# A decoder layer's projection weights laid out by the host in chunks of 256 columns, and a sixth raw buffer for them

## The chip, the cores and the metric

The kernel runs on one core of one Trainium2 chip. The metric is device time in microseconds (us), the median of several executions. Engine names are those of the profile: PE does the matmuls (PEld loads their stationary operand), DVE, ACT and POOL work on tiles, SP issues plain DMAs, and POOL issues the indirect DMAs (the gathers). SPq and POOLq are the queues of these issues.

## What is computed

One decoder layer for 512 tokens of width 1024, cut to what matters here:

```python
z = rmsnorm(x) @ w_in                    # 1024 x 3592, split into:
# ml_qk 1024 | ml_v 512 | ml_o 512 | ml_i 4, ml_f 4 | da_q 512 | da_k 512 | da_v 512
h = concat([mlstm_heads(...), diff_attention_heads(...)])     # 4 heads of each
x = x + h @ w_out
# cross-attention into a memory of 256 rows
q = rmsnorm(x) @ w_cq;  k = mem_n @ w_ck;  v = mem_n @ w_cv
x = x + softmax(q k^T / 16) v @ w_co
# PEER: each token takes 16 of 16384 experts for each of 8 heads
q = rmsnorm(x) @ w_pq;  sc = q . sub_keys;  eidx, gate = product_key_top16(sc)
x = x + sum_k gate_k * gelu(h . peer_u[eidx_k]) * peer_v[eidx_k]
out = rmsnorm(x)
```

All of w_out, w_cq, w_ck, w_cv, w_co and w_pq are 1024 x 1024, in float32.

## The kernel before

The tokens are four blocks of 128. The program runs in groups:

- The **first group** is block 0 alone, up to about 220 us: input projection (`proj_feat` and `proj_tok` with `w_in`; tiles qkg, vg, og, dag, dvg), mLSTM and attention, `mem_front` (keys and values of the memory; tiles mkw, mvw), output projection (wog), cross-attention (cqt, co0) and the PEER query (pq0).
- The **second group** is `mixers(1, 3, ...)`, blocks 1 to 3 together, from about 226 to 640 us. Beside it block 0's experts are fetched and reduced: POOL gathers rows of `peer_u` and `peer_v` (512 KB each, tiles u and v), and DVE takes the dot products with u and the weighted sums of v. `feed` mixes them into the projections.
- The **tail** (640 to some 800 us) does cross-attention and the PEER query for blocks 2, 3 and 1; routing follows. From 1000 us on, blocks 2 and 3 go through all experts as dense matmuls (tiles ud, vd, of 512 and 256 KB), block 1 by gathers.

The projection weights are read from HBM as the model stores them, rows of the full matrix. `w_parts` (line 337) brings one chunk of 256 columns in two halves of 512 KB, [128 partitions, 4, 256], where each partition gets 4 runs of 1 KB that lie a whole matrix row apart, 128 rows each. The raw halves go round a ring of buffers, `rings["wr"]`: 5 in the first group, 3 in the second. A load of a half can be issued once the half that was in its buffer has been used. Where a product is split for precision, ACT casts the half to a rounded H (line 346), DVE or POOL subtract it for L (line 330), and PE runs three matmuls for one (lines 314 to 316); elsewhere PE multiplies the raw half (line 322). In the tail `w_chunk` (line 219) brings a chunk of 1 MB at once, 8 runs of 1 KB for each partition, in another ring.

All these loads, the loads of constants and of x, and the stores of intermediate results to HBM go through SP's one queue, in order. The constants of `setup_small` are among them: lt (line 254) holds the four lambda vectors, each broadcast to 128 partitions; its two products ljunk (line 258) run on DVE ahead of eo (line 510). The memory's values are stored in mv_d (line 446).

The order on each engine is not written out by hand. The framework's scheduler builds it, from dependencies, free buffers and its own estimate of durations; the program only gives the order in which instructions are handed to it, and rings of buffers.

Of the kernel before, what the change touches and what calls it, by code (L numbers as in the profile page):

```python
# [19 lines left out]
P = 128  # L20
S = 512
D = 1024
ND = 8
# [64 lines left out]
def layer_kernel(ctx, tc, x, mem, norm_mix_g, w_in, conv_w, b_igate, b_fgate, ml_norm_g,  # L88
                 lambda_q1, lambda_k1, lambda_q2, lambda_k2, da_norm_g, w_out, norm_ca_g,
                 norm_mem_g, w_cq, w_ck, w_cv, w_co, norm_ffn_g, w_pq, sub_keys, peer_u, peer_v,  # L90
                 final_norm_g, peer_ut, out):

# [1 line left out]

    nc = tc.nc
    xf = x[0]
    w_in, w_out, w_cq, w_ck, w_cv, w_co, w_pq = (a[0] for a in (w_in, w_out, w_cq, w_ck, w_cv, w_co, w_pq))
    uf = peer_u[0]  # L100
    vf = peer_v[0]
    outf = out[0]
# [17 lines left out]
    def pa(name):  # L120
        return psums[1](name)
# [46 lines left out]
    mp = fctx.enter_context(tc.tile_pool(name="mixers", bufs=1, side="right"))  # L168
    actx = ExitStack()
    home = [actx.enter_context(tc.tile_pool(name="first", bufs=1, side="right"))]  # L170
    rings = {"big": 4, "wr": 5, "wH": 2, "wL": 2}

    def ft(shape, tag, name, bufs=2, dt=F32):
        return home[0].tile(shape, dt, tag=tag, name=name, bufs=bufs)
# [39 lines left out]
    def w_tile(shape, name):  # L214
        return ft(shape, "w", name, bufs=rings["w"])

    def w_chunk(src, c0, name):
        t = w_tile([P, ND, 256], name)
        nc.sync.dma_start(t, src[:, c0:c0 + 256].rearrange("(k p) c -> p k c", p=P))
        return t  # L220

    def load_x(src, T0, NT, name):
# [14 lines left out]
    cols = bp.tile([P, 64], F32, name="cols")  # L237
    nc.vector.tensor_copy(cols, cps[:, :64])
    wg = mp.tile([P, ND, 8], F32, name="wg")
    nc.sync.dma_start(wg, w_in[:, 2048:2056].rearrange("(k p) c -> p k c", p=P))  # L240
    wgs = tuple(mp.tile([P, ND, 8], F32R, name=f"wg{hl}") for hl in "HL")
    put(wgs, wg)

# [82 lines left out]
    def low(dst, src, high):  # L326
        kind = LOW[min(lows[0], len(LOW) - 8 + lows[0] % 8)] if group[0] else LOW_FIRST[lows[0] % 8]
        lows[0] += 1
        e = nc.gpsimd if kind == "pool" else nc.vector
        e.tensor_sub(dst, src, high.bitcast(F32))  # L330

    def w_parts(src, c0, name, split):

        for q in range(2):
            sh = [P, 4, 256]
            raw = ft(sh, "wr", f"{name}_{q}", bufs=rings["wr"])
            nc.sync.dma_start(raw, src[q * 512:(q + 1) * 512, c0:c0 + 256].rearrange("(k p) c -> p k c", p=P))
            if not split:
                yield range(4 * q, 4 * q + 4), raw
                continue  # L340
            if group[0] or rings["wH"] and lows[0] % 2:
                H = ft(sh, "wH", f"{name}H{q}", bufs=rings["wH"], dt=F32R)
            else:
                H = keep.tile(sh, F32R, tag="hv", name=f"{name}H{q}", bufs=2)
            L = ft(sh, "wL", f"{name}L{q}", bufs=rings["wL"], dt=F32R)
            nc.scalar.copy(H, raw)
            low(L, raw, H)
            yield range(4 * q, 4 * q + 4), (H, L)
# [43 lines left out]
    def proj_feat(src, c0, nf, T, n, name, evac, parts=w_parts):  # L392

        for c in range(nf // 2):
            o = [pa(f"{name}o{c}{j}") for j in range(2)]
            for ks, w in parts(src, c0 + c * 256, f"{name}w{c}", T.split):
                for j in range(2):
                    for k in ks:
                        product(o[j][:, :n], at(w, slice(None), k - ks[0], slice(j * P, (j + 1) * P)), T(k),
                                k == 0, k == ND - 1)  # L400
                    if ks[-1] == ND - 1:
                        evac(2 * c + j, o[j][:, :n])
            feed("proj", n // P)

    def proj_tok(src, c0, n, T, NT, name, evac, parts=w_parts):

        for c in range(0, n, 256):
            o = [pa(f"{name}o{c}_{tt}") for tt in range(NT)]
            for ks, w in parts(src, c0 + c, f"{name}w{c}", T.split):
                for tt in range(NT):  # L410
                    for k in ks:
                        product(o[tt][:, :256], T(k, slice(tt * P, (tt + 1) * P)), at(w, slice(None), k - ks[0]),
                                k == 0, k == ND - 1)
                    if ks[-1] == ND - 1:
                        evac(tt, c, o[tt][:, :256])
            feed("proj", NT)
# [38 lines left out]
    def mixers(T0, NT, hT):  # L455
        G = NT * P
        g = f"g{T0}_"
# [100 lines left out]
        def ev_da(f, o):  # L558
            if f < 4:
                nc.scalar.mul(daqT[:, f, :], o, -0.125)  # L560
            else:
                nc.scalar.copy(dakT[:, f - 4, gl], o)
        proj_feat(w_in, 2056, 8, hT, G, f"da{g}", ev_da)

        def ev_dv(tt, c, o):
            nc.scalar.copy(dav[:, T0 + tt, c:c + 256], o)
        proj_tok(w_in, 3080, 512, hT, NT, f"dv{g}", ev_dv)

        mix = big([P, NT, D], f"mix{g}")

# [483 lines left out]
    for tt in range(NDENSE):  # L1054
# [3 lines left out]
        for t4 in range(0, P, 4):  # L1058
# [9 lines left out]
            for q in range(4):  # L1068
                g = tr[:, 2, t4 + q:t4 + q + 1]
# [8 lines left out]
            c0 = tt * P + t4  # L1078
# [18 lines left out]
    for tt in range(NDENSE):  # L1097
        for q in range(2):
            f = half("uH", f"h3d{tt}{q}", 4)
# [81 lines left out]
    with tc.manual_schedule(engines={mybir.EngineType.PE, mybir.EngineType.DVE, mybir.EngineType.Activation,  # L1181
# [25 lines left out]
_INS = ["x", "mem", "norm_mix_g", "w_in", "conv_w", "b_igate", "b_fgate", "ml_norm_g", "lambda_q1", "lambda_k1",  # L1207
        "lambda_q2", "lambda_k2", "da_norm_g", "w_out", "norm_ca_g", "norm_mem_g", "w_cq", "w_ck", "w_cv", "w_co",
        "norm_ffn_g", "w_pq", "sub_keys", "peer_u", "peer_v", "final_norm_g"]
# [26 lines left out]
```

## Time and profile before

| | before |
|---|---|
| median of 3 runs | 1842.48 us (1842.26 to 1842.88) |
| profiled execution | 1843.16 us |
| its span | 1841.3 us |
| mean granted clock of TensorE | 0.927 |
| busy: PE, DVE, POOL, ACT | 86%, 79%, 59%, 44% |
| DMA over the span | 501.14 MB, 272 GB/s mean |
| SP's queue / the gathers' queue | 36.4% / 42.6% of the DMA engines' time |

The span is what the trace covers, from its first to its last instruction; 1.9 us of the profiled execution lie outside it, and this execution stands 0.7 us above the median. Busy shares are averages over stages that are limited by different things, so no share says by itself what a change in one stage is worth.

### The profile page before, as it was taken

What the parts mean: (1) busy time and instruction counts of PE and PEld (TensorE: products, weight loads), DVE (VectorE), ACT (ScalarE), POOL (GpSimd) and SP (SyncE); (2) the same over time, 40 slices, a digit from 0 to 9 for tenths busy, and PEclk for the clock granted to TensorE, in tenths of its full rate; (3) what the DMA queues carried; (4) which work ended last, traced back from release to release, by engine and by line L of the source; (5) the groups of instructions that cost most, each with busy time, mean ns of one, the idle gap of its engine ahead of it and who ended that gap; (6) DMA issues with size and microseconds to landing.
All of it is one profiled execution on the core that took longest, in us unless ns stands there. A gap on an engine that the chain in (4) does not pass through costs nothing.

```text
span 1841.3 us, 27663 instructions
## 1 busy us (share of the span) xinstructions
PE 1584.1 (86%) x9223; PEld 1323.4 (72%) x9223; DVE 1453.5 (79%) x3042; ACT 805.0 (44%) x1835; POOL 1077.2 (59%) x864
## 2 busy tenths in 40 slices
PE   7898796887755799899977999999999999999986
PEld 6798685776334668774666877777777877777775
DVE  4354399878999848889786888888889888888874
ACT  3454423435432112236998444444444444444433
POOL 2000127788888727114343777777777778777754
PEclk9999878988557899999998999999999999999998
DMA  7758615888888998417566999999999999999983
GB/s 237 247 183 275 229 35 162 279 273 309 275 279 277 352 377 315 148 42 248 171 214 209 335 336 337 335 337 320 333 331 337 332 327 338 335 328 330 329 318 111
DMA packets 211455, 501.14 MB, mean 272 GB/s; under 512 B 20792, under 2 KB 90480, under 8 KB 210544
## 3 DMA queue, kind: packets, MB, share of 16 engines
q0 software_dynamic: 74304, 270.57, 42.6%
q1 hardware_dynamic: 137008, 228.82, 36.4%
q8 instruction: 72, 1.18, 0.3%
q14 instruction: 71, 0.58, 0.1%
HBM read 490.93 MB, written 8.39 MB: 271 GB/s over the span
## 4 chain that ended last, share of the span: by engine, by line
DVE 25%; issue 15%; POOL 13%; PE 11%; DMA 10%; ACT 10%; POOLq 2%; DVEq 0%; ACTq 0%
DMA vd<-in_peer_v_dram 8%; POOL vL L1140 5%; DVE u L968 5%; POOL u L906 4%; DVE uL L1131 3%; ACT vH L1139 3%; PE cqt_o L322 2%; POOL v L906 2%; DVE vaccp L995 2%; ACT oi L1071 2%; POOLq L1140 2%; ACT uH L1130 2%; ACT oj L1067 1%; DMA u<-in_peer_u_dram,eidx 1%; ACT W L1079 1%
## 5 line engine op out<-in xcount | busy, mean ns | idle before, releaser
L906 POOL DMA_INDIRECT v<-in_peer_v_dram,eidx x256 | 289.1, 1129 | 249.3 <-PE vpe L989 61.9
L906 POOL DMA_INDIRECT u<-in_peer_u_dram,eidx x256 | 318.9, 1246 | 144.0 <-DVE u L968 59.8
L1131 DVE TENSOR_TENSOR uL<-ud,uH 128x512 fp32r<-128x512 f32 x256 | 312.8, 1259 | 114.3 <-ACT uH L1130 111.9
L1140 POOL TENSOR_TENSOR vL<-vd,vH 128x512 fp32r<-128x512 f32 x256 | 352.6, 1396 | 55.0 <-ACT vH L1139 35.5
L314 PE MATMUL ua<-hH,uH 128*128 128x256 f32 x1024 | 290.2, 283 | 3.1 <-ACT hH L1103 3.1
L315 PE MATMUL ua<-hL,uH 128*128 128x256 f32 x1024 | 290.7, 284 | 0.2 <-DVE hL L1104 0.2
L316 PE MATMUL ua<-hH,uL 128*128 128x256 f32 x1024 | 290.6, 284 | 0.0
L315 PE MATMUL acc<-vL,pH 128*128 128x512 f32 x512 | 223.7, 437 | 51.5 <-POOL vL L1140 48.5
L1160 ACT CAST pH<-ua 128x256 fp32r<-128x256 f32 x128 | 47.8, 374 | 405.7 <-DVE ua L1158 405.7
L314 PE MATMUL acc<-vH,pH 128*128 128x512 f32 x512 | 203.4, 397 | 9.4 <-ACT vH L1139 9.4
L316 PE MATMUL acc<-vH,pL 128*128 128x512 f32 x512 | 203.2, 397 | 0.0
L314 PEld LDWEIGHTS ua<-hH,uH 128*128 128x128 f32 x1024 | 196.8, 192 | 8.8 <-ACT hH L1103 3.3
L315 PEld LDWEIGHTS ua<-hL,uH 128*128 128x128 f32 x1024 | 196.9, 192 | 5.8 <-DVE hL L1104 0.5
L316 PEld LDWEIGHTS ua<-hH,uL 128*128 128x128 f32 x1024 | 196.9, 192 | 0.0
L315 PEld LDWEIGHTS acc<-vL,pH 128*128 128x128 f32 x512 | 97.1, 190 | 130.3 <-POOL vL L1140 115.9
L968 DVE SCALAR_TENSOR_TENSOR u<-u,h3k 128x1024 f32<-128x1024 f32 x112 | 158.8, 1429 | 24.4 <-DMA u<-in_peer_u_dram,eidx 24.1
L1139 ACT CAST vH<-vd 128x512 fp32r<-128x512 f32 x256 | 154.1, 623 | 44.4 <-DMA vd<-in_peer_v_dram 36.7
L995 DVE SCALAR_TENSOR_TENSOR vaccp<-v,gate,vaccp 128x1024 f32<-128x1024 f32 x127 | 162.1, 1277 | 0.2
L968 DVE SCALAR_TENSOR_TENSOR u<-u,h3p 128x1024 f32<-128x1024 f32 x128 | 154.1, 1207 | 0.0
L1130 ACT CAST uH<-ud 128x512 fp32r<-128x512 f32 x256 | 145.9, 617 | 0.7 <-DVE hL L1104 0.7
L995 DVE SCALAR_TENSOR_TENSOR vacc<-v,gate,vacc 128x1024 f32<-128x1024 f32 x83 | 107.9, 1300 | 15.7 <-DMA v<-in_peer_v_dram,eidx 15.1
L314 PEld LDWEIGHTS acc<-vH,pH 128*128 128x128 f32 x512 | 97.8, 191 | 27.2 <-ACT vH L1139 9.8
(643 smaller groups left out, 3401.9 us busy)
## 6 DMA issues: line engine op xcount, KB each, us to landing
ud<-in_peer_ut_dram SPq DMA_DIRECT2D x128, 512.0 KB
vd<-in_peer_v_dram SPq DMA_DIRECT2D x256, 256.0 KB
qkg_w<-in_w_in_dram SPq DMA_DIRECT2D x16, 512.0 KB
dag_w<-in_w_in_dram SPq DMA_DIRECT2D x16, 512.0 KB
wog_w<-in_w_out_dram SPq DMA_DIRECT2D x16, 512.0 KB
vg_w<-in_w_in_dram SPq DMA_DIRECT2D x8, 512.0 KB
og_w<-in_w_in_dram SPq DMA_DIRECT2D x8, 512.0 KB
dvg_w<-in_w_in_dram SPq DMA_DIRECT2D x8, 512.0 KB
```

Of the source, the lines that this page charges most:

```text
L314: nc.tensor.matmul(o, lhsT=l[0], rhs=r[0], start=start, stop=False)
L315: nc.tensor.matmul(o, lhsT=l[0], rhs=r[1], start=False, stop=False)
L316: nc.tensor.matmul(o, lhsT=l[1], rhs=r[0], start=False, stop=stop)
L322: nc.tensor.matmul(o, lhsT=l, rhs=r, start=start, stop=stop)
L906: g = nc.gpsimd.indirect_dma_start(out=u, out_offset=None, in_=src, in_offset=bass.IndirectOffsetOnAxis(ap=eidx[:, s:s + 1], axis=0))
L968: nc.vector.scalar_tensor_tensor(u, u, 1.0, h3, op0=OP.mult, op1=OP.mult, accum_out=act[:, s:s + 1])
L995: nc.vector.scalar_tensor_tensor(acc, v, c, acc, op0=OP.mult, op1=OP.add)
L1130: nc.scalar.copy(H, r[:, sl])
L1131: nc.vector.tensor_sub(L, r[:, sl], H.bitcast(F32))
L1139: nc.scalar.copy(H, v)
L1140: nc.gpsimd.tensor_sub(L, v, H.bitcast(F32))
L1160: nc.scalar.copy(H, a)
```

## The change

The host lays out the seven projection weights anew: as [chunk of 256 columns][partition][k][256 columns]. Half a chunk is then one run of 4 KB for each partition, a whole chunk one of 8 KB. The eight gate columns of `w_in`, which stand in the middle of it, become an input of their own, `w_gates`, so that what follows begins at a multiple of 256. In the first group the ring of raw halves gets a sixth buffer; the second group's stays at 3. Byte counts, tiles, casts and matmuls are the same.

```diff
-    w_in, w_out, w_cq, w_ck, w_cv, w_co, w_pq = (a[0] for a in (w_in, w_out, w_cq, w_ck, w_cv, w_co, w_pq))
...
-    rings = {"big": 4, "wr": 5, "wH": 2, "wL": 2}
+    rings = {"big": 4, "wr": 6, "wH": 2, "wL": 2}
...
     def w_chunk(src, c0, name):
         t = w_tile([P, ND, 256], name)
-        nc.sync.dma_start(t, src[:, c0:c0 + 256].rearrange("(k p) c -> p k c", p=P))
+        nc.sync.dma_start(t, src[c0 // 256])
...
-    nc.sync.dma_start(wg, w_in[:, 2048:2056].rearrange("(k p) c -> p k c", p=P))
+    nc.sync.dma_start(wg, w_gates)
...
             raw = ft(sh, "wr", f"{name}_{q}", bufs=rings["wr"])
-            nc.sync.dma_start(raw, src[q * 512:(q + 1) * 512, c0:c0 + 256].rearrange("(k p) c -> p k c", p=P))
+            nc.sync.dma_start(raw, src[c0 // 256, :, 4 * q:4 * q + 4, :])
...
-        proj_feat(w_in, 2056, 8, hT, G, f"da{g}", ev_da)
+        proj_feat(w_in, 2048, 8, hT, G, f"da{g}", ev_da)
...
-        proj_tok(w_in, 3080, 512, hT, NT, f"dv{g}", ev_dv)
+        proj_tok(w_in, 3072, 512, hT, NT, f"dv{g}", ev_dv)
...
+    w_in = _np.asarray(inputs["w_in"])[0]
+    laid["w_in"] = w_in[:, list(range(2048)) + list(range(2056, w_in.shape[1]))][None]
+    for name in ("w_in", "w_out", "w_cq", "w_ck", "w_cv", "w_co", "w_pq"):
+        laid[name] = _np.asarray(laid[name])[0].reshape(ND, P, -1, 256).transpose(2, 1, 0, 3)
+    laid["w_gates"] = w_in[:, 2048:2056].reshape(ND, P, 8).transpose(1, 0, 2)
```

Since the scheduler builds the order anew, the change also moves instructions. Three places follow. The first is SP's queue in the first group, where the last halves of og and the first of dag are loaded; lt are the four lambda vectors. Before:

```order
L337 DMA og0_w0_0_468<-in_w_in_dram 128x4x256
L337 DMA og0_w0_1_474<-in_w_in_dram 128x4x256
L254 DMA lt_438<-in_lambda_q1_dram 128x64
L254 DMA lt_438<-in_lambda_k1_dram 128x64
L254 DMA lt_438<-in_lambda_q2_dram 128x64
L254 DMA lt_438<-in_lambda_k2_dram 128x64
L337 DMA og0_w256_0_483<-in_w_in_dram 128x4x256
L337 DMA og0_w256_1_489<-in_w_in_dram 128x4x256
```

And of the change:

```order
L336 DMA og0_w0_0_468<-in_w_in_dram 128x1024
L336 DMA og0_w0_1_474<-in_w_in_dram 128x1024
L336 DMA og0_w256_0_483<-in_w_in_dram 128x1024
L253 DMA lt_438<-in_lambda_q1_dram 128x64
L253 DMA lt_438<-in_lambda_k1_dram 128x64
L253 DMA lt_438<-in_lambda_q2_dram 128x64
L253 DMA lt_438<-in_lambda_k2_dram 128x64
L336 DMA og0_w256_1_489<-in_w_in_dram 128x1024
```

One more half of weights stands ahead of the four small loads. It is so along the whole first group: each constant and each store that SP issues there now has one more half ahead of it (one of wog_w768 ahead of mv_d, too). On PE, the transposes skp1 (line 272, which wait for eo) now stand three matmuls later, behind two more of og0_w0_1 and one of og0_w256_0.

The second place is ACT in the second group, at the gates of og (gsigg, a sigmoid) and the first mLSTM blocks (dmg, an exponential). ACT loads a table whenever it goes from one kind of function to the other. Before:

```order
L346 CAST og1_w256H1_3502<-og1_w256_1_3500 128x1024
L540 ACT_TABLE_LOAD
L540 ACTIVATE acg1_7_3138<-acg1_7_3138 128x384
L541 ACTIVATE kT_135<-acg1_7_3138 128x384
L346 CAST dag1_w0H0_3561<-dag1_w0_0_3559 128x1024
L594 ACT_TABLE_LOAD
L594 ACTIVATE dmg1_00_4049<-mbg1_0_4045,eo1_2536 128x128
L594 ACTIVATE dmg1_00_4049<-mbg1_0_4045,eo2_2549 128x128
L554 ACT_TABLE_LOAD
L554 ACTIVATE gsigg1_0_3350<-og1_o256_0_3455 128x256
```

And of the change:

```order
L593 ACTIVATE dmg1_00_4049<-mbg1_0_4045,eo3_2563 128x128
L553 ACT_TABLE_LOAD
L553 ACTIVATE gsigg1_0_3350<-og1_o256_0_3455 128x256
L591 ACT_TABLE_LOAD
L591 ACTIVATE dmg1_01_4059<-dmg1_01_4059,eo1_2536 128x128
L593 ACTIVATE dmg1_01_4059<-mbg1_0_4045,eo2_2549 128x128
L593 ACTIVATE dmg1_01_4059<-mbg1_0_4045,eo3_2563 128x128
L553 ACT_TABLE_LOAD
L553 ACTIVATE gsigg1_1_3351<-og1_o256_1_3456 128x256
L553 ACTIVATE gsigg1_2_3352<-og1_o256_2_3457 128x256
```

Gates and exponentials alternate more often: ACT has 21 table loads in the second group where it had 18.

The third place is POOL in the second group, between gathers (tiles u0) and the L of a weight half of dag. Before:

```order
L906 DMA u0_31_2754<-in_peer_u_dram,eidx0_2210 128x1024
L906 DMA u0_32_2757<-in_peer_u_dram,eidx0_2210 128x1024
L330 TENSOR_TENSOR dag1_w2L0_3706<-dag1_w2_0_3703,dag1_w2H0_3705 128x1024
```

And of the change:

```order
L905 DMA u0_31_2754<-in_peer_u_dram,eidx0_2210 128x1024
L905 DMA u0_32_2757<-in_peer_u_dram,eidx0_2210 128x1024
L905 DMA u0_33_2760<-in_peer_u_dram,eidx0_2210 128x1024
L329 TENSOR_TENSOR dag1_w2L0_3706<-dag1_w2_0_3703,dag1_w2H0_3705 128x1024
```

The subtraction stands behind one gather more. Line numbers of the change are one lower than before.

## Rows read from the trace of the kernel before

**Rows 1.** Windows by stage: us, busy PE, PEld, DVE, ACT, POOL (instructions), PEclk, DMA share, GB/s.
```profile
24.00:80.00 56.00, 52.62 (x355) 47.28 (x353) 21.75 (x94) 22.78 (x51) 0.57 (x2) 1.00 0.87 268
...
300.00:640.00 340.00, 235.19 (x1226) 190.06 (x1227) 299.70 (x546) 123.46 (x296) 274.75 (x183) 0.74 0.84 287
...
1000.00:1841.00 841.00, 771.63 (x4586) 649.73 (x4585) 702.04 (x902) 359.11 (x771) 626.48 (x514) 0.99 0.91 319
```

**Rows 2.** Two shorter windows, same columns.
```profile
50.00:70.00 20.00, 19.03 (x150) 18.16 (x149) 0.85 (x2) 3.50 (x11) 0.00 (x0) 1.00 0.97 301
1000.00:1400.00 400.00, 373.99 (x2230) 314.32 (x2230) 340.92 (x505) 173.90 (x374) 309.99 (x254) 1.00 0.94 332
```

**Rows 3.** PE's waits up to 231 us: us in total, times, longest.
```profile
PE skp L272 <- DVE eo L510: 1.1, 1, 1.1
...
PE dag_o L322 <- DMA dag_w<-in_w_in_dram: 1.0, 2, 0.7
PE wog_o L315 <- DVE wog_w768L L330: 0.9, 1, 0.9
```

**Rows 4.** PE's groups, 24 to 60 us: count, busy, mean ns, idle before.
```profile
L322 PE MATMUL og_o<-og_w,hT 128*128 128x256 f32 x32 | 7.5, 382 | 0.0
...
L322 PE MATMUL dag_o<-hT,dag_w 128*128 128x128 f32 x56 | 6.9, 278 | 1.0 <-DMA dag_w<-in_w_in_dram 1.0
```

**Rows 5.** Timeline of SP's issues from 34 us: start, us, what.
```profile
35.41 2.10 SPq L337 DMA_DIRECT2D og_w<-in_w_in_dram  x2
...
40.91 0.43 SPq L254 DMA_DIRECT2D lt<-in_lambda_k_dram  x1
41.44 0.93 SPq L337 DMA_DIRECT2D og_w<-in_w_in_dram  x2
```

**Rows 6.** Timeline of DVE, 42 to 50 us, in brackets idle before.
```profile
46.36 0.23 DVE L258 SCALAR_TENSOR_TENSOR ljunk<-lt 128x64 f32<-128x64 f32 x1 [2.41 <-DMA lt<-in_lambda_k_dram]
...
47.13 0.28 DVE L510 COPY eo<-ep 128x128 f32<-128x128 f32 x1
```

**Rows 7.** Timelines of SP, ACT, DVE and PE, 140 to 150 us.
```profile
140.12 0.34 SPq L446 DMA_DIRECT2D mv_d<-mv  x1
140.92 2.00 SPq L337 DMA_DIRECT2D wog_w<-in_w_out_dram  x2
146.97 1.05 ACT L346 CAST wog_w768H<-wog_w 128x1024 fp32r<-128x1024 f32 x1 [3.36 <-DMA wog_w<-in_w_out_dram]
148.05 1.22 DVE L330 TENSOR_TENSOR wog_w768L<-wog_w,wog_w768H 128x1024 fp32r<-128x1024 f32 x1 [1.23 <-ACT wog_w768H L346]
149.33 0.38 PE L315 MATMUL wog_o<-wog_w768L,mixTg_H 128*128 128x256 f32 x1 [0.88 <-DVE wog_w768L L330]
```

**Rows 8.** DVE's waits, 226 to 436 us.
```profile
DVE u L968 <- DMA u<-in_peer_u_dram,eidx: 16.2, 9, 3.4
DVE dag_w3L L330 <- ACT dag_w3H L346: 6.2, 2, 4.4
```

**Rows 9.** Timelines in the second group: one table load, one gather on POOL.
```profile
340.36 1.28 ACT L554 ACT_TABLE_LOAD   x1
391.80 1.77 POOL L906 DMA_INDIRECT u<-in_peer_u_dram,eidx  x1 [0.16 <-issue]
```

**Rows 10.** DMA queues, 640 to 660 us: packets, MB, share (q0 gathers, q1 SP).
```profile
q0 software_dynamic: 1132, 4.11, 52.6%
q1 hardware_dynamic: 2020, 3.84, 51.2%
```

**Rows 11.** The same, 660 to 690 us.
```profile
q1 hardware_dynamic: 6015, 6.06, 62.5%
q0 software_dynamic: 1351, 4.88, 43.4%
```

**Rows 12.** PE's waits, 640 to 800 us.
```profile
PE pqt_o L322 <- DMA pqt_w<-in_w_pq_dram: 2.0, 2, 1.1
```

More of the change, by code (lines that the diff above doesn't have):

```diff
@@ L90, in layer_kernel @@
                  norm_mem_g, w_cq, w_ck, w_cv, w_co, norm_ffn_g, w_pq, sub_keys, peer_u, peer_v,
-                 final_norm_g, peer_ut, out):
+                 final_norm_g, peer_ut, w_gates, out):
     nc = tc.nc
     xf = x[0]
-    w_in, w_out, w_cq, w_ck, w_cv, w_co, w_pq = (a[0] for a in (w_in, w_out, w_cq, w_ck, w_cv, w_co, w_pq))
     uf = peer_u[0]
@@ L1224 @@
     laid["peer_ut"] = _np.asarray(inputs["peer_u"]).reshape(P, P, ND, P).transpose(0, 3, 2, 1).reshape(P, P, D)
-    for name in _INS + ["peer_ut"]:
+    w_in = _np.asarray(inputs["w_in"])[0]
[3 more added lines that the diff above has]
+    laid["w_gates"] = w_in[:, 2048:2056].reshape(ND, P, 8).transpose(1, 0, 2)
+    for name in _INS + ["peer_ut", "w_gates"]:
         a = _np.ascontiguousarray(laid[name])
```

## Prediction

> **What bounds the kernel now.** I read the windows by stage first [rows 1]. From 24 to 80 us PE is busy 52.6 of 56 us, so there it is PE that weights have to wait for. From 300 to 640 us it is DVE, 299.7 of 340 us, with POOL at 274.8 and the DMA engines at 0.84 of their time. In the dense stretch, 841 us of the 1841, PE is at 92% and no projection weight is loaded. So the change can act on about half the kernel, and there only where an engine stands waiting for a weight, or for a transfer that stands behind one.
>
> Then the speed. In a stretch of the first group that moves nothing but weights in 1 KB runs, 301 GB/s at a DMA share of 0.97 are 310 GB/s for a full share; in the dense stretch, with rows of 2 and 4 KB, 332 at 0.94 are 353 [rows 2]. A half of 524,288 bytes takes 1.69 us at the first speed and 1.49 at the second: 0.2 us less for each, if 4 KB runs reach 353.
>
> Against this stands how fast PE eats them [rows 4]. A half of og is 4 matmuls, which the trace records as two each: 32 records are 4 halves in 7.5 us, 1.88 us a half. PE needs longer for a half than even the old layout (1.69 us). So the transfers set the pace only where something has put them behind, and PE's waits in the first group say where: 1.1 us at skp, 1.0 us in two waits for dag_w, 0.9 us at wog_w768L [rows 3]. Its longer waits there are for norms and transposes, which no weight changes.
>
> **The change part by part.** The sum is made against the profiled execution, 1843.16 us, of which 1841.3 are span; it stands 0.7 us above the median.
>
> *Wait at skp: 0.* The four lt loads wait in SP's queue for a buffer, and go out between 39.6 and 41.3 us, behind og's first halves [rows 5]. The last product of them runs at 46.36, after 2.41 us of waiting, and eo, for which skp waits, is next on DVE, at 47.13 [rows 6]. The sixth buffer lets one more half go ahead of lt, and lt land up to 1.5 us later (1.49 us from above). But skp also stands three og matmuls further back on PE, 3 × 2 × 7.5/32 = 1.4 us. Both ends: the wait of 1.1 goes altogether, if the extra half passes while the queue would idle (the half is issued in the 2 us in which SP waited, 37.5 to 39.6); or it grows by 0.1, and a little more, if PE comes there sooner. I take no change, since the two shifts are equal.
>
> *Waits for dag_w: −1.0.* These come a few us after the queue stood behind lt: og's last halves go out at 41.44, after it, and everything behind is that much late [rows 5]. One more half in hand is worth 1.88 us of PE's time, more than the longest of the two waits (0.7), and each half that follows comes 0.2 us sooner. The other end is 0.
>
> *wog_w768: −0.7.* SP issues the store mv_d, 1 MB, at 140.12, and the last two halves of wog after it at 140.92; ACT waits 3.36 us for the first of them, casts from 146.97, DVE subtracts from 148.05 and PE starts at 149.33 after 0.88 us of waiting [rows 7]. In the change the first half goes ahead of mv_d and comes early enough. The second stays behind mv_d, whose transfer is now pushed back by part of that half, so a little of the wait may return there. From −0.9 to 0; I take −0.7, near the full wait, since two halves are together 0.4 us shorter.
>
> *Second group: −1.5.* It loads 36 halves, 18.9 MB: 61.0 us at 310 GB/s, 53.5 at 353. That is 7.4 us of the DMA engines' time, the most that can be had; nothing is the least. What of it reaches the end is read from DVE, which bounds this group: while the weights are loaded, it waits 16.2 us in nine waits for gathered rows of u [rows 8]. If each of those has one half in front of it, it shortens by 0.2 us, 1.8 together. Some have none, and the v gathers at the group's end wait beside a few more; I take 1.5. Its other large wait, 6.2 us for dag_w3H, is ACT's cast coming late and no transfer.
>
> *At nothing.* The start (PE's first matmuls wait for norms), the gates' own load (32 KB), and the remaining 70-odd halves of the first group: hidden behind PE's 1.88 us a half. The 12 loads of 1 MB in the tail: PE waits 2.0 us for pqt_w [rows 12], but route, which follows it, runs on DVE, and DVE is not short of these; at most 2.0 are gained. The sixth buffer itself adds no instruction.
>
> *The new order: taken at 0.* ACT has three table loads more in the second group, 1.28 us each, and a subtraction for dag stands behind one gather more, 1.77 us on POOL [rows 9]: 3 × 1.28 + 1.77 = 5.6 us if all lies on the path. ACT is busy only 123.5 of 340 us there [rows 1], so the loads are likely covered by its idle time; without that cover they delay gates and exponentials for which DVE waits. Other moves go the other way; between 0 and 5.6 I take 0.
>
> Sum: 0 − 1.0 − 0.7 − 1.5 = −3.2, so 1840.0 for an execution like the profiled one, and 1839.3 us on the scale of the median.
>
> **A rule weighed.** The rows give 310 GB/s for 1 KB runs and 353 for longer ones [rows 2], which is the whole reason for any gain by layout. The Trainium skill, "DMA: Bandwidth & Descriptors", section "Specifications", says that transfers reach line rate from 512 B on; by that the old runs of 1 KB were as fast as any and the layout saves nothing. The trace agrees only in part: 310 is 12% short of 353.
>
> **The rivals.**
>
> *Nothing measurable, 1842.5.* The two speeds may not be a matter of run length: the stretch at 353 GB/s also reads other tensors and has gathers beside it. In 660 to 690 us, where 6015 of 7366 packets are weights in 1 KB runs, the queues moved 10.9 MB in 30 us, 365 GB/s at a share of 1.06, 344 for a full share [rows 11]: the gap to 353 is then 3%, and the layout gives 36 × 0.04 = 1.4 us of DMA time. With lt as late as bounded above and the new order costing a little, the first group's 1.7 us are given back. The 512 B rule above would make it so.
>
> *A larger gain, 1830.1.* All bounds on the good side: skp 1.1, dag 1.0, wog 0.9, second group 7.4, pqt 2.0, together 12.4 us off 1843.16, less 0.7. For it speaks that DVE and the DMA engines are both nearly full from 300 to 640 us [rows 1]; against it that weights flow in only a part of that time, and that u waits there are 16.2 us in all.
>
> *The new order costs, 1844.9.* The forecast's −3.2 and the 5.6 us of table loads and the gather ahead of dag's L, all on the path.
>
> *Slower: longer packets crowd out the gathers, 1852.9.* Weights and gathers share the DMA engines on two queues. If the engines take turns by packet, then 1 KB packets beside a gather's 4 KB leave the gather four fifths of the speed, and 4 KB packets leave it half. A gather of 0.5 MB beside weights then takes 0.524/(353/2) = 2.97 us in place of 0.524/(353 × 4/5) = 1.86, 1.1 us more. DVE's nine waits for u, and two more at the end of the group, would each grow by it: 12.1 us, less the 1.7 us of the first group. It decides from the point where 1.1 us exceeds the slack of a gather, and those nine have none. What speaks against it is measured: beside SP packets of 1.9 KB on average (3.84 MB in 2020), some of them intermediate results read back in long runs, the gathers moved 4.11 MB in 20 us, 206 GB/s [rows 10]; beside 1 KB packets 4.88 MB in 30 us, 163 GB/s [rows 11]. Longer packets did not take from them. The Trainium skill, same page, section "Queues, rings and completion order", has the engines take turns by packet, each of some 9 to 17 descriptors; the trace does not show that this favours the longer runs.
>
> **How the numbers follow.** A difference of 0.2%, 3.7 us, is about what a measurement of this kernel can tell from none: faster means below 1838.8, slower above 1846.2. Chances: the forecast 0.44, with 1836 to 1842 around it (by the bounds of dag, wog, u and skp), of which 0.18 lie below 1838.8; larger gain 0.23, all faster; nothing 0.14; the order's cost 0.10, half of it beyond 1846.2 since more was moved than I priced; crowding 0.09, slower. So faster 0.41, same 0.26 + 0.14 + 0.05 = 0.45, slower 0.14. The range 1830 to 1846 leaves out half of the larger gain (0.11), and the crowding (0.09).
>
> **What would show it.** Right: no wait of PE for dag_w, and under 0.3 us at wog_w768L; the window 50 to 70 us at more GB/s for a share; u's waits up to 436 us nearer 14 than 16 us; a dense stretch that only starts earlier. Wrong: skp's wait well over 1.2 us, which would say that lt pays for the extra half; u's waits grown by some us, with weights beside them; ACT table loads that DVE waits for in the second group. A gain in the dense stretch itself would be none of mine.

## The result: slower by half a per cent

The changed kernel takes 1853.69 us, the median of 11 runs (1851.26 to 1859.88), against 1843.05 us for the kernel before (11 runs, 1833.91 to 1852.9). The ratio is 1.0051, with a 95% interval of 1.0035 to 1.0067. Forecast were 1839.3 us, and a range up to 1846. Single executions lie up to 10 us from the median of these two kernels, so ratios with their intervals count below, and a profile is one draw from that spread. One execution of the kernel before, in the session of e5 to e8, was slow (3339.62 us) and counts in no ratio. The profiled execution of the changed kernel took 1857.56 us, 3.9 over its median.

The windows by stage of the changed kernel, which answer to [rows 1]:

```profile
24.00:80.00 56.00, 51.06 (x335) 46.48 (x333) 19.59 (x86) 18.62 (x47) 0.92 (x3) 0.94 0.71 244
...
300.00:640.00 340.00, 227.23 (x1227) 189.87 (x1225) 291.68 (x546) 125.24 (x297) 270.64 (x173) 0.75 0.80 274
1000.00:1841.00 841.00, 771.96 (x4614) 653.23 (x4614) 696.85 (x905) 368.14 (x789) 617.23 (x509) 0.99 0.91 319
```

From 24 to 80 us fewer bytes move (244 for 268 GB/s), PE does 20 matmuls fewer, and its clock is below full for a part of the time. PE's waits of the changed kernel up to 231 us, and its timeline from 44 us, say where (answering to [rows 3]):

```profile
PE skp L271 <- DVE eo L509: 4.9, 1, 4.9
...
PE wog_o L314 <- DVE wog_w768L L329: 0.8, 1, 0.8
```

```profile
44.54 2.76 PE L321 MATMUL og_o<-og_w,hT 128*128 128x256 f32 x12
52.22 1.12 PE L271 MATMUL skp<-ident,skr 128*128 128x128 f32 x4 [4.92 <-DVE eo L509]
53.12 5.65 PE L321 MATMUL og_o<-og_w,hT 128*128 128x256 f32 x14
58.61 1.61 PE L321 MATMUL dag_o<-hT,dag_w 128*128 128x128 f32 x13
```

The waits for dag_w are gone, but the one at skp has grown from 1.1 to 4.9 us. Behind it 14 records of og take 5.65 us, 0.40 each, where 12 took 2.76 before it, 0.23 each: having stood still for 4.9 us, PE works on at the lower clock. From 52 to 58 us of the changed kernel the granted clock (the column before the DMA share) is 0.50, the lower of the two levels, 1.2 GHz:

```profile
52.00:58.00 6.00, 5.79 (x16) 4.80 (x17) 0.77 (x3) 2.54 (x4) 0.00 (x0) 0.50 0.92 336
```

DVE's timeline of the changed kernel, answering to [rows 6], has the cause of the wait:

```profile
51.11 0.23 DVE L257 SCALAR_TENSOR_TENSOR ljunk<-lt 128x64 f32<-128x64 f32 x1 [4.48 <-DMA lt<-in_lambda_k_dram]
...
51.88 0.28 DVE L509 COPY eo<-ep 128x128 f32<-128x128 f32 x1
```

The last lt row is used at 51.11 us, not 46.36. The DMA engines' view from 34 to 54 us, in slices of 0.5 us (busy tenths, then GB/s), shows why; first the kernel before, then the changed one:

```profile
DMA  9958799999999311101001479999999999998999
GB/s 379 381 186 84 131 350 375 369 369 379 363 348 332 102 45 38 43 14 33 19 17 48 137 233 385 387 389 371 354 346 346 352 350 348 391 410 348 354 369 365
```

```profile
DMA  8965798789779633320000002234449989999999
GB/s 328 377 262 164 238 311 238 262 328 352 270 229 344 270 152 130 96 49 10 13 22 4 22 22 62 63 124 148 98 107 328 311 312 394 434 410 385 410 418 426
```

While the four lt loads (128 KB together) go through, the engines move next to nothing: some 5 us below 140 GB/s before (from 40.5 us), some 7 us below 150 GB/s after (from 42 us). Weights wait behind them in SP's queue.

Later marks in these two traces: PE's first matmul of the second group (qkg) is at 227.99 us before and 237.70 after; its first for cqt_w, the start of the tail, at 637.06 and 654.31; the first dense matmul at 994.31 and 1008.01. The spans differ by 13.4 us (1854.7 and 1841.3), so in these two executions all of it arises before the dense stretch: 9.7 us in the first group and 7.5 in the second, of which some 3.6 come back during the tail.

### The profile page after: what moved, and what is told of

It is laid out like the page before. It is cut to its first block, busy times and chain, and to the rows that moved or that the text cites. A ratio compares the mean times of both kernels' runs of the same rounds, so it can differ in the third digit from the quotient of the medians.

```text
span 1854.7 us, 27670 instructions
## 1 busy us (share of the span) xinstructions
PE 1577.6 (85%) x9223; PEld 1324.3 (71%) x9223; DVE 1443.6 (78%) x3042; ACT 808.3 (44%) x1838; POOL 1068.6 (58%) x864
## 3 DMA queue, kind: packets, MB, share of 16 engines
q1 hardware_dynamic: 82352, 228.82, 34.7%
## 4 chain that ended last, share of the span: by engine, by line
DVE 22%; DMA 18%; ACT 12%; issue 12%; PE 11%; POOL 9%; POOLq 0%; DVEq 0%; ACTq 0%
DMA vd<-in_peer_v_dram 14%; DVE u L967 5%; POOL vL L1139 4%; ACT vH L1138 4%; DVE uL L1130 4%; DMA u<-in_peer_u_dram,eidx 3%; PE cqt_o L321 2%; DVE vaccp L994 2%; ACT oi L1070 2%; ACT uH L1129 2%; POOL u L905 2%; POOL v L905 2%; ACT oj L1066 1%; DVE ua L1157 1%; PE pqt_o L321 1%
## 5 line engine op out<-in xcount | busy, mean ns | idle before, releaser
L905 POOL DMA_INDIRECT u<-in_peer_u_dram,eidx x256 | 324.7, 1268 | 148.9 <-DVE u L967 61.1
L1130 DVE TENSOR_TENSOR uL<-ud,uH 128x512 fp32r<-128x512 f32 x256 | 306.6, 1235 | 119.9 <-ACT uH L1129 117.1
L1139 POOL TENSOR_TENSOR vL<-vd,vH 128x512 fp32r<-128x512 f32 x256 | 347.2, 1374 | 53.8 <-ACT vH L1138 35.4
L967 DVE SCALAR_TENSOR_TENSOR u<-u,h3k 128x1024 f32<-128x1024 f32 x112 | 147.1, 1325 | 28.0 <-DMA u<-in_peer_u_dram,eidx 27.9
L994 DVE SCALAR_TENSOR_TENSOR vacc<-v,gate,vacc 128x1024 f32<-128x1024 f32 x83 | 108.9, 1312 | 21.0 <-DMA v<-in_peer_v_dram,eidx 20.3
```

The costliest lines, as they stand in the source:

```text
L905: g = nc.gpsimd.indirect_dma_start(out=u, out_offset=None, in_=src, in_offset=bass.IndirectOffsetOnAxis(ap=eidx[:, s:s + 1], axis=0))
L967: nc.vector.scalar_tensor_tensor(u, u, 1.0, h3, op0=OP.mult, op1=OP.mult, accum_out=act[:, s:s + 1])
L994: nc.vector.scalar_tensor_tensor(acc, v, c, acc, op0=OP.mult, op1=OP.add)
L1130: nc.vector.tensor_sub(L, r[:, sl], H.bitcast(F32))
L1139: nc.gpsimd.tensor_sub(L, v, H.bitcast(F32))
```

## The experiments

The scheduler turned out not to see the layout: with the same ring, the orders of both layouts are the same in all rows of PE, DVE, ACT and POOL, and on SP but for the gates' load. Order and layout can thus be tried apart. All ratios are to the kernel before in the same session, with 95% intervals; a ratio is not quite the quotient of the two medians given with it (e13: 1.0055, and 1853.39/1846.2 = 1.0039).

| run | ring | new layout | lambda | ratio | interval |
|---|---|---|---|---|---|
| the change | 6 | all | one row | 1.0051 | 1.0035 to 1.0067 |
| e1 | 5 | all | one row | 1.0037 | 1.0021 to 1.0052 |
| e17 (e1 anew) | 5 | all | one row | 1.0035 | 1.0021 to 1.0049 |
| e2 | 6 | none | one row | 1.0005 | 0.9988 to 1.0022 |
| e6 | 5 | w_in | one row | 1.0024 | 1.0005 to 1.0044 |
| e7 | 5 | all but w_in | one row | 1.0053 | 1.0033 to 1.0073 |
| e18 (e7 anew) | 5 | all but w_in | one row | 1.0035 | 1.0015 to 1.0054 |
| e9 | 5 | tail alone | one row | 1.0005 | 0.9990 to 1.0020 |
| e10 | 5 | tail, runs of 1 KB | one row | 1.0001 | 0.9986 to 1.0016 |
| e5 | 5 | none | spread | 0.9994 | 0.9976 to 1.0013 |
| e8 | 5 | w_in | spread | 1.0001 | 0.9979 to 1.0023 |
| e11 | 5 | all but the tail | spread | 1.0015 | 1.0000 to 1.0031 |
| e12 | 5 | all but w_in | spread | 1.0006 | 0.9991 to 1.0022 |
| e4 | 5 | all | spread | 1.0007 | 0.9992 to 1.0023 |
| e3 | 6 | all | spread | 1.0018 | 1.0003 to 1.0034 |

### Layout or order: e1 and e2

```diff
# e1: the changed kernel, with
-    rings = {"big": 4, "wr": 6, "wH": 2, "wL": 2}
+    rings = {"big": 4, "wr": 5, "wH": 2, "wL": 2}
# e2: the kernel before, with
-    rings = {"big": 4, "wr": 5, "wH": 2, "wL": 2}
+    rings = {"big": 4, "wr": 6, "wH": 2, "wL": 2}
```

> The new layout with the ring of 5. The scheduler builds the order of before for it (all rows of POOL, ACT, DVE and PE alike; on SP only the gates' load differs), so run length alone is tested. Theory O, that the order built for six buffers costs the time (lt behind one more half, the second group's new order): 1838 to 1843, no slower than before, PE waits at skp 1 to 2 us. Theory L, that longer packets cost it (gathers crowded out, or the four lt rows slower beside 4 KB runs): slower by most of the change's 10 us, 1849 to 1854, with skp near 5 us if it is lt and DVE's waits for u up if it is the gathers.

> The old layout with the ring of 6. Its order is that of the changed kernel on every engine (again but for the gates' load), so the order and the sixth buffer are tested alone. Theory O: 1849 to 1856, slower than before by some 10 us, skp waits near 5 us. Theory L: 1841 to 1845, as before, skp 1 to 2 us.

Measured: 1852.17 us and 1846.9 us, before 1845.18. The loss comes with the layout, and the order built for six buffers costs nothing that can be measured in the total (its interval ends at 1.0022). Theory O falls. In the profile of e1, which has the order of before, PE waits at skp nearly as long as in the changed kernel, and in that of e2 not:

```profile
PE skp L271 <- DVE eo L509: 4.5, 1, 4.5
```

```profile
PE skp L272 <- DVE eo L510: 1.7, 1, 1.7
```

### The four rows of lambda: e3, e4, e5

lt is loaded by reading one row of 256 bytes 128 times, once for each partition. In these runs the host gives each vector as 128 equal rows; shapes and orders stay.

```diff
-            nc.sync.dma_start(lt[:, r, :], row_bcast(l, 64))
+            nc.sync.dma_start(lt[:, r, :], l)
...
+    for name in ("lambda_q1", "lambda_k1", "lambda_q2", "lambda_k2"):
+        laid[name] = _np.tile(_np.asarray(laid[name]).reshape(1, 64), (P, 1))
```

> The changed kernel, but the host gives the four lambda vectors already spread over 128 partitions, so that lt's loads read 128 rows in place of one row 128 times. Order unchanged. If lt are slow because all partitions read one row, the wait at skp falls from 4.9 us to under 1, PE's clock does not fall behind it, and the first group gets 5 to 7 us of its 8 back: 1846 to 1849. If lt are late because of what stands ahead of them in the queue, or because small loads are slow there whatever they read, nothing moves: 1851 to 1855, skp 4 to 5 us.

> New layout, ring of 5 (the order of before), lambda spread by the host. Theory O with lt slow by their one row: faster than before by the 1.1 us at skp and the 1.0 at dag and what the layout brings, 1836 to 1841. Theory L (gathers): slower than before by what e1 is.

> The kernel before (old layout, ring of 5, same order), with lambda spread by the host. Theory Q, that 4 KB runs beside them make the four one-row loads of lt slow: the old layout lost only the 1.1 us at skp and 1.0 at dag_w to them, so 0 to 3 us below before, 1842 to 1845. Rival R, that lt's slowness is lt's own and comes and goes between executions whatever the layout: spreading gives here what it gave with the new layout, 4 to 5 us, 1840 or 1841.

Measured: 1849.03 us with the changed kernel, 1847.49 with layout and ring of 5 (before 1845.18), 1845.6 with the kernel before (before 1846.74). With the new layout the rows' spreading gives back 0.3%, from 1.0051 to 1.0018 and from 1.0037 to 1.0007; with the old one 0.06%, which is not to be told from nothing (its interval leaves room for 0.24%). No wait at skp is left in their profiles. DVE's timeline of e4, as [rows 6]:

```profile
45.07 0.23 DVE L257 SCALAR_TENSOR_TENSOR ljunk<-lt 128x64 f32<-128x64 f32 x1 [0.99 <-DMA lt<-in_lambda_k_dram]
...
45.84 0.28 DVE L509 COPY eo<-ep 128x128 f32<-128x128 f32 x1
```

and its DMA engines from 34 to 54 us, which never stand idle:

```profile
DMA  7877868759798878876968999999997689999976
```

### Which weights: e6, e7, e8, e12

Each of the seven matrices can be given in either layout; the loads take the one or the other form by the shape of their source.

```diff
+            if len(src.shape) == 4:
+                part = src[c0 // 256, :, 4 * q:4 * q + 4, :]
+            else:
+                part = src[q * 512:(q + 1) * 512, c0:c0 + 256].rearrange("(k p) c -> p k c", p=P)
+            nc.sync.dma_start(raw, part)
...
+    for name in ("w_in",):        # e6, e8; the other six in e7, e12
```

> Ring of 5, only w_in in the new layout; the halves around lt have 4 KB runs, the tail's chunks stay in 1 KB runs. Theory Q: skp waits 4 to 5 us and the time is 4 to 7 us over before, 1849 to 1852; DVE's waits for v between 226 and 700 us stay at 10 to 13 us. Rival C, that the gathers at the end of the second group pay beside longer packets: most of the loss is gone, 1845 to 1847.

> Ring of 5, w_in in the old layout, the other six in the new one. Theory Q alone: as before, 1844 to 1847, skp 1 to 2 us. Rival C: DVE's waits for v between 226 and 700 us at 17 to 21 us in place of 10 to 13, and the time 3 to 5 us over before, 1848 to 1850.

> Ring of 5, only w_in in the new layout, lambda spread. Both suspected costs are out and the layout's gain is left for the first 440 us: theory Q and rival C together give 1841 to 1845, no slower than the old layout with lambda spread. Over 1847 there is a cost of long runs in the mixers that neither names.

> As e7 (all but w_in in the new layout, ring of 5), lambda spread. If e7's 9 us are the tail's, nothing moves but the 1 us that spreading gave in the old layout: 1852 to 1856. If they were lt's in part, it falls to e4's, 1846 to 1849.

Measured: 1850.55, 1856.06 and 1845.75 us (before 1846.74), and 1846.87 (before 1846.57). The times of e6 and e8 are as theory Q has them: w_in's 4 KB runs cost 0.24%, and nothing once the rows are spread, though the two intervals overlap. The wait is not: the profile of e6 (1846.37 us) has skp at 2.3 us, not 4 to 5. e7 contradicts theory Q: w_in's loads, which alone stand near lt, are in the old form there, and yet it is as slow as the changed kernel; spreading takes its loss away too (e12). Its profile (1852.42 us) shows a skp of only 1.8 us.

### The tail's gathers: e9 and e10

The chunks of the tail come from copies (t_cq, t_co, t_pq), all else is in the old layout. In e10 each run of 256 columns is followed by 8 unused ones, so that a chunk lies in one place but comes in runs of 1 KB.

```diff
-        proj_feat(w_cq, 0, ND, cT, G, f"cq{g}", ev_q, parts)
+        proj_feat(t_cq if group[0] else w_cq, 0, ND, cT, G, f"cq{g}", ev_q, parts)
...
+        w = w.reshape(ND, P, -1, 256).transpose(2, 1, 0, 3)
+        w = _np.concatenate([w, w[..., :8]], axis=3)      # e10 alone
```

> The kernel before (old layout, ring of 5, same order), but the tail's 12 chunks of 1 MB, and they alone, come from a copy in the new layout, in runs of 8 KB. Theory C, that the engines take turns by packet and 8 KB packets crowd out the gathers of v: DVE's waits for v between 226 and 700 us 17 to 21 us in place of 10 to 13, the gathers at 140 GB/s or so in the first 20 us of cqt in place of 195, the time 3 to 9 us over before, 1848 to 1855. Rival: the loss of all but w_in is elsewhere (wog, x, the first group), then 1843 to 1847 here and v as before.

> As e9, but a chunk's rows are padded by 8 columns each, so that the chunk still lies in one place of HBM and yet comes in runs of 1 KB. Theory C: run length alone decides, so waits for v 10 to 13 us, gathers at 195 GB/s, time as before, 1843 to 1847. If the place in HBM decides (chunk in one stretch), as e9.

Measured: 1847.21 and 1847.66 us, before 1846.57. The DMA queues from 640 to 660 us, as [rows 10], first e9, then e10:

```profile
q1 hardware_dynamic: 745, 5.45, 65.9%
q0 software_dynamic: 793, 2.89, 35.7%
```

```profile
q0 software_dynamic: 1234, 4.53, 58.5%
q1 hardware_dynamic: 2243, 3.36, 46.3%
```

and DVE's waits for v from 226 to 700 us, in the kernel before, e9, e10 and the changed kernel:

```profile
DVE vacc L995 <- DMA v<-in_peer_v_dram,eidx: 12.5, 11, 2.5
```

```profile
DVE vacc L1000 <- DMA v<-in_peer_v_dram,eidx: 17.5, 11, 2.5
```

```profile
DVE vacc L1000 <- DMA v<-in_peer_v_dram,eidx: 12.6, 12, 2.5
```

```profile
DVE vacc L994 <- DMA v<-in_peer_v_dram,eidx: 17.9, 10, 2.5
```

So the crowding is real: beside weights in 8 KB runs the gathers move 2.89 MB in 20 us, 145 GB/s, beside 1 KB runs 4.53 MB, 227 (4.11 and 206 in the kernel before, [rows 10]). It goes by the length of a run, not by where the chunk lies. DVE waits 5 us longer for v. But the time does not move measurably: in its profile e9's tail begins at 639.38 us, 2.3 after that of the kernel before, and its interval leaves room for at most 0.2%, 3.7 us.

These two profiles show something else, which bears on lt. Both kernels have the old layout everywhere in the first group, and PE waits longer at skp than in the kernel before and than in e6 (first e9, then e10):

```profile
PE skp L273 <- DVE eo L515: 2.9, 1, 2.9
```

```profile
PE skp L273 <- DVE eo L515: 3.5, 1, 3.5
```

e10's profiled execution (1847.68 us) stands at its median, and e10 is no slower than the kernel before. So waits of 1.1 to 3.5 us occur at skp in the old layout too, without a loss in the time.

### Both out: e11

All of w_parts' loads in the new layout, the tail in the old one, rows spread.

```diff
+    for name in ("cq", "co", "pq"):          # copies in the old layout, for the tail's chunks
+        w = _np.asarray(inputs["w_" + name])[0]
+        laid["t_" + name] = w[None]
```

> Ring of 5, order of before: all of w_parts' loads in the new layout, the tail's chunks in the old one, lambda spread. Both costs that the runs point to (lt, the gathers of v) are out. Theory Q with C: no slower than before, 1841 to 1846, waits for v 10 to 13 us. Over 1848: 4 KB runs cost something in w_out, w_cq, w_ck, w_cv, w_co or w_pq of the first two groups.

Measured: 1848.27 us, before 1846.57, ratio 1.0015. This is the layout where it was to help, with both known costs out, and it is not faster. DVE's waits for v are at 15.0 us, not 10 to 13. No version here beats the kernel before by more than the noise.

### The price of a one-row load: e13 to e16

Eight more loads of lambda rows stand ahead of lt; what they bring is not used. The four kernels have the same order among themselves, but on DVE, ACT and POOL it is another one than that of the kernel before. So they can be compared with each other; their ratios to the kernel before contain this order, which was not tried alone.

```diff
+        lx = ft([P, 8, 64], "ac", "lx", bufs=2)
+        for r in range(8):
+            nc.sync.dma_start(lx[:, r, :], row_bcast((lambda_q1, lambda_k1, lambda_q2, lambda_k2)[r % 4], 64))
...
+            nc.sync.dma_start(lx[:, r, :], l_spread[r % 4])      # e16 in place of the line above
```

> The kernel before with eight more loads of the lambda rows (each broadcast to 128 partitions) right ahead of lt; what they bring is not used. 12 one-row loads take 3 x 5.4 = 16 us in place of 5.4 if their price is their own, PE's wait at skp grows by about 11 us to 12, and the time by 10 to 14 us, 1855 to 1860. If the loads run together, less.

> The same eight loads in the kernel with the new layout and the ring of 5. Theory Q, that 4 KB runs around them make one-row loads slower: 12 loads take 24 to 28 us and the time stands 17 to 22 us over before, 6 to 10 us over e13. Rival R, that their time varies by itself: as e13, within 3 us.

> The same in the kernel with all but w_in in the new layout. Around these loads it is the kernel before, so by theory Q as by rival R the 12 loads take what they take in e13, and the time is e13's plus what the tail costs (0 to 3 us). If it stands 8 us or more over e13, e7 was no accident and its price is tied to the one-row loads in a way that no neighbour in the queue explains.

> As e14, but the eight added loads read rows that the host has spread over 128 partitions; lt itself still reads one row. If one row is what costs, the added eight take under 4 us together and the time is e1's plus 2 to 4 us, 1853 to 1857. If small loads cost as such, as e14.

| run | layout | added | us | ratio | interval |
|---|---|---|---|---|---|
| e13 | old | 8 one-row | 1853.39 | 1.0055 | 1.0036 to 1.0073 |
| e15 | all but w_in | 8 one-row | 1854.69 | 1.0051 | 1.0034 to 1.0069 |
| e14 | all | 8 one-row | 1859.79 | 1.0080 | 1.0060 to 1.0101 |
| e16 | all | 8 spread | 1847.24 | 1.0006 | 0.9992 to 1.0019 |

A one-row load has a price of its own in any layout. On DVE's timelines the second ljunk, which needs the last lt, runs at 56.60 us in e13 and 59.55 in e14, after the first load was issued at 39.73 and 39.30: 16.9 us for 12 loads in the old layout, 20.3 in the new one, 1.4 and 1.7 each. In e16, with eight spread and four one-row loads, it is at 50.33, 10.9 us after the issue at 39.41. Theory Q asked for 24 to 28 us in e14, which stays far below. Nor do these profiles show that the layout around them lengthens the loads: in e15, with the same 1 KB runs around them as e13, the twelve take 18.4 us (39.34 to 57.72), midway between e13 and e14. The times of e13 and e15 are alike (1.0055 and 1.0051), so here the layout of all but w_in costs nothing.

e16 came out below its forecast (1853 to 1857 us). Its scheduler placed eo ahead of ljunk on DVE, as in all four:

```profile
42.17 0.29 DVE L512 COPY eo<-ep 128x128 f32<-128x128 f32 x1 [1.32 <-PE ep L510]
...
50.33 0.23 DVE L260 SCALAR_TENSOR_TENSOR ljunk<-lt 128x64 f32<-128x64 f32 x1 [3.40 <-DMA lt<-in_lambda_k_dram]
```

Here lt is one row, the layout is new, lt's last row comes as late as ever, skp does not wait for it, and the ratio is 1.0006. That alone does not show that skp was the way to the loss. In its profile PE waits for weights instead (2.2 us for og_w, 1.2 for dag_w), the second group begins at 236.63 us, as late as in e1 (236.81), and the time is made up later: from there to the first dense matmul it is 762.3 us, 769.6 in e1, and 761.0 to 764.1 in all four kernels of this order. In e13 PE waits for the weights behind the loads, and longer:

```profile
PE og_o L325 <- DMA og_w<-in_w_in_dram: 8.8, 1, 8.8
```

### The same programs loaded anew: e17 and e18

> The kernel of e1 unchanged, loaded anew. If its 1.0037 belongs to the program: 1.002 to 1.005. If it belongs to where a session puts the inputs, or to chance: 1.001 or less, as with spread rows.

> The kernel of e7 unchanged, loaded anew. If its 1.0053 belongs to the program: 1.004 to 1.007. If e15 reads it rightly and it was the session: 1.000 to 1.002, the tail's gathers alone.

Measured: 1.0035 and 1.0035 (1852.72 and 1852.64 us, before 1847.46). Both losses belong to the programs, and not to a session; e18's lies below its forecast of 1.004. Each profiled execution here was the fastest of its kernel, 1844.5 and 1848.16 us. For e17 that fits lt: the same program as e1, with skp at 2.1 us in place of 4.5 and the tail's start at 642.41 us in place of 648.81.

```profile
PE skp L271 <- DVE eo L509: 2.1, 1, 2.1
```

## Why the prediction was wrong

**The step that failed** is the one at skp, which I had put down as "0", with a growth of 0.1 as the bad end. It grew by 3.8 us in the profile, from 1.1 to 4.9, and PE's lower clock behind it took some 14 × (0.40 − 0.23) = 2.4 us more; og's last matmul ends 6.3 us later (58.77 us, and 52.44 before). I had priced only how many bytes stand ahead of lt. That part was nearly right: e2, which has the extra half ahead and the old layout, waits 1.7 us; e1, without the extra half, 4.5. So the sign that I had named, a wait at skp well over 1.2 us, came, but not because of the extra half. What sets its landing is how long the four one-row loads themselves take in the queue, and this was in the trace of before (the idle stretch from 40.5 us) and in [rows 5, 6]: 5.4 us from the last issue to its use, for 32 KB. With spread rows the wait is gone, in each of four pairs of kernels with the new layout 0.2 to 0.5% come back, and only 0.06% in the old one. That the loss needs both the rows and the new layout is what the pairs show. That eo behind ljunk is the way from lt to this wait of PE, the waits show. That this wait is the whole loss of the program is not shown: e9 and e10 wait 2.9 and 3.5 us there and lose nothing, e6, e7 and e18 wait 1.8 to 2.3 and are slower, and e16 does not decide. A kernel with eo placed ahead of ljunk, and nothing else changed, was not tried.

**Why lt's one-row loads cost time only with the new layout** stays open. From the issue of the first lt to the second ljunk it is 3.2 to 5.0 us in the six profiles with spread rows, 6.8 to 9.1 in the six with one row and w_in in 1 KB runs (before, e2, e7, e9, e10, e18), and 7.8, 7.9, 10.1 and 10.7 in the four with w_in in 4 KB runs (e17, e6, e1, the change). So what one row costs is plain in either layout; the two ranges with one row overlap, and executions of one program differ as much (e1 and e17). What the profiles of the first group do show is the sum: PE's first matmul for wog is at 135.8 to 136.9 us with spread rows, at 136.7 to 140.0 in those six, at 137.8 in e6, and at 140.2 to 144.1 in the three with one row and all weights in the new layout (e17, e1, the change). All but w_in is the least explained: 1.0053 and 1.0035 in two loadings, 1.0006 with spread rows, no cost in e15 against e13, no w_in in 4 KB runs near lt, and skp at 1.8 us and wog at 137.6 and 137.9 in its two profiles. Nothing that the traces show near lt explains it. Spread rows are larger inputs and may also shift the place of other inputs in HBM; whether this matters was not tried.

**Dag, −1.0: the wait went, the gain did not.** In the changed kernel PE comes there late enough not to wait. With spread rows, where it is not late, there is no wait with six buffers (e3) and one of 0.5 us with five (e4), so the step itself may have been right; in the time it does not show.

**wog_w768, −0.7: measured −0.1.** The first half came early, as forecast. The 0.8 us that are left are no transfer's: ACT casts the first half from 151.21 us, but DVE subtracts it only from 154.03, after two subtractions for wog_w512 and one addition, and PE waits for that. The second half, behind mv_d, was not late either; ACT's cast of it stood waiting for an H buffer, as its timeline in the changed kernel shows:

```profile
155.43 1.05 ACT L345 CAST wog_w768H<-wog_w 128x1024 fp32r<-128x1024 f32 x1 [3.18 <-PE wog_o L314]
```

**Second group, −1.5: not there.** The transfers did become cheaper. SP's queue moves the same 228.82 MB in 82352 packets for 137008, and in 34.7% of the engines' time for 36.4%, which is 644 for 670 us. The page of the changed kernel:

```profile
q0 software_dynamic: 74304, 270.57, 42.6%
q1 hardware_dynamic: 82352, 228.82, 34.7%
```

A stretch of the first group that moves weights alone, 60 to 80 us of the changed kernel, answers to [rows 2]:

```profile
60.00:80.00 20.00, 20.00 (x150) 18.89 (x149) 1.23 (x1) 4.28 (x11) 0.00 (x0) 1.00 0.81 279
```

279 GB/s at a share of 0.81 are 344 for a full share, where 1 KB runs had 310 and I had taken 353. So a half is 0.17 us shorter, and no engine's end depends on it (PE is busy all of these 20 us): PE needs 1.88 us for a half in the first group, and in the second the gathers, not the weights, are late. DVE's waits for u up to 446 us, which were to carry this term, in the changed kernel, e1, e17 and e2:

```profile
DVE u L967 <- DMA u<-in_peer_u_dram,eidx: 11.9, 7, 3.8
```

```profile
DVE u L967 <- DMA u<-in_peer_u_dram,eidx: 15.4, 7, 4.0
```

```profile
DVE u L967 <- DMA u<-in_peer_u_dram,eidx: 16.7, 7, 3.7
```

```profile
DVE u L968 <- DMA u<-in_peer_u_dram,eidx: 6.4, 2, 3.9
```

Before it was 16.2 [rows 8]. With the order of before (e1, e17) the new layout leaves them where they were; with the order of six buffers they fall in the old layout too (e2). e8, e11, e12 and e4, with the rows spread, are at 1.0001 to 1.0015, where the old layout with spread rows is at 0.9994.

**Order, 0: right in the total** (e2, 1.0005), and the rival built on it falls; but the way there was not as I had it, and that it comes to nothing is luck. The three profiles with the order of six buffers (the change, e2, e3) take 416.6 to 420 us from the first matmul of the second group to the start of the tail, the thirteen with the order of before 405.3 to 413.8. DVE waits there for two casts and one activation (dncg) of ACT for which it hardly waits in the kernel before; in e2:

```profile
DVE dvg_w256L L330 <- ACT dvg_w256H L346: 3.8, 2, 3.6
DVE dncg L611 <- ACT dncg L610: 3.3, 1, 3.3
DVE dvg_w0L L330 <- ACT dvg_w0H L346: 3.0, 1, 3.0
```

The tail gives most of it back: from its start to the first dense matmul it is 350.7 to 353.8 us in these three, and 355.6 to 360.7 in the thirteen. What makes it shorter was not looked for. (The 18 and 21 table loads named with the change are those of the whole program; in the second group ACT has 9 and 12. The three more are right.)

**Crowding: the mechanism was right where I had argued it away, and its price was wrong.** That the rival's 1852.9 us lies near the measured time is chance: the waits for u on which it was built did not grow (above), and where the gathers do pay, beside the tail's 8 KB runs, e9, which has nothing but this, is at 1.0005. My argument against it, 206 GB/s beside long packets and 163 beside short ones [rows 10, 11], compared two stretches in which the gathers were not asked for equally. At one place in the program and one time (e9 and e10) it is 145 against 227. In e9 793 gather packets of 3.6 KB on average go beside 745 weight packets of 7.3 KB, nearly one for one. So they do in the kernel before, in the first 10 us of the very stretch of [rows 11], 660 to 670 us, where the gathers get 307 GB/s beside packets of 1 KB:

```profile
q0 software_dynamic: 844, 3.07, 78.6%
q1 hardware_dynamic: 845, 0.85, 24.5%
```

The Trainium skill, "DMA: Bandwidth & Descriptors", section "Queues, rings and completion order", has engines take turns between queues by packet. The trace agrees in these two windows, where the profile counts each run as a packet; in others it is not one for one (2243 to 1234 in e10), and whether both queues then had packets waiting is not shown.

## What to carry to other kernels

Before making a transfer faster, find the instruction that ends later because of it. Here weights in 4 and 8 KB runs took 4% less of the engines' time for SP's bytes, and nothing of it reached the time. Look in the trace for stretches in which the DMA engines stand idle while a queue is full: a few small loads that read one row for all partitions can hold back everything behind them, and also, through an in-order engine, work that has nothing to do with them. Giving the rows already spread took that stretch away here; in the time it brought 0.2 to 0.5% with the new layout and nothing measurable with the old one. Placing the consumer of such a load behind the work that others wait for is the other thing to try; here it was not tried by itself. And take more than one profile before a wait is called the cause: here one program showed 4.5 and 2.1 us at the same place.

## What was not expected of the hardware

- Loading one row of 256 bytes to 128 partitions takes 1.4 us in the queue when twelve follow each other (e13), with the engines nearly idle; when the 128 rows are apart, the engines stay busy with what is around (e4).
- Two queues can share the engines packet for packet (844 to 845 in 10 us before, 793 to 745 in 20 us of e9), so the longer run gets more: the gathers got 145 GB/s beside packets of 8 KB and 227 beside those of 1 KB (e9, e10).
- Executions of one program differ by up to 10 us from their median (1833.91 to 1852.9 us for the kernel before), once by 14 (1866.89 in e18), and two profiles of one program by 10.6 us (e1 and e17).
